# The first y tile of an interleave kernel: loaded by the store queue, issued ahead of the opening barrier

## Chip, cores, metric

The kernel runs on one core of one Trainium2 chip. The metric is the device time of one execution in microseconds (us), lower is better. All runs told of here were with a TensorE clock of 1.0 (TensorE does nothing in this kernel). Verdicts use a margin of 2%; several questions below are smaller than that, and for them the 95% interval of the ratio is given.

## The reference

```python
# x, y: float32 [32, 256, 1024]
result = np.zeros((32, 256, 2048), dtype=np.float32)
result[..., 0::2] = x
result[..., 1::2] = y
```

x and y are 33.55 MB each, the output 67.11 MB. There is no arithmetic: 134.2 MB are moved.

## The kernel before

The tensors are seen as flat. One tile is 128 partitions x 8192 floats (4.19 MB); there are eight of x and eight of y, in two buffers each. VectorE writes x into the even and y into the odd columns of an output tile, which is half as wide in inputs (4096 of each) and so is 4.19 MB too; there are sixteen, in two buffers. SP issues the loads, ACT the stores. The list of transfers that one issuing engine has handed over is called its queue or ring (q1 is SP's and q10 ACT's in the pages); both feed the same 16 DMA engines. A packet is what one DMA engine moves at a time, here a row of 32 KB. The opening barrier is the point where all engines wait for each other before the program's body.

```python
xpool = ctx.enter_context(tc.tile_pool(name="xp", bufs=2))
ypool = ctx.enter_context(tc.tile_pool(name="yp", bufs=2))
opool = ctx.enter_context(tc.tile_pool(name="op", bufs=2))
...
zero = wpool.tile([16, 128], fp32, name="zero")
nc.vector.memset(zero, 0.0)
first = dataclasses.replace(of, offset=0, ap=[[2 * WL, 16], [1, 128]])
nc.scalar.dma_start(out=first, in_=zero)          # the tiny write, 8 KB

for lw in lwidths:                                # 8 tiles
    ...
    nc.sync.dma_start(out=xtile, in_=xs)
    nc.sync.dma_start(out=ytile, in_=ys)
    soff = 0
    while soff < lw:                              # 2 output tiles
        ...
        nc.vector.tensor_copy(out=otile[:, 0::2], in_=xsub)
        nc.vector.tensor_copy(out=otile[:, 1::2], in_=ysub)
        nc.scalar.dma_start(out=os_, in_=otile)
        soff += width
```

After the program is built, the first x load is moved by hand into the program's opening block, ahead of SP's part of the opening barrier, so that it starts before the engines have met:

```python
at, moved = next((b, i) for b in blocks[1:] for i in b.instructions
                 if i.engine == mybir.EngineType.SP and i.opcode == "DMACopy")
assert not moved.sync_info.on_wait
... # take it out of its block
opening.insert(gate, moved)      # gate: SP's Drain in the opening block
```

The tiny write touches bytes that the first store overwrites; the first store waits for it.

## Time and profile before

| | before |
|---|---|
| time, median of 3 runs | 316.41 us (315.72 to 316.87) |
| span of the profiled run | 313.8 us |
| bytes moved, mean rate over the span | 134.23 MB, 428 GB/s |
| VectorE busy | 72.8 us, 23% |
| first store issued | 24.32 us after the span's start |

"Span" runs from the first to the last instruction on the device; it is about 1.8 us shorter than the time. A row of digits gives the busy tenths in 40 equal slices, 9 for 90% or more. In a timeline, "[11.25 <-DMA xtile<-in_x_dram]" says that the engine stood idle for 11.25 us and that the landing of this load ended it. A DMA's row stands at its issue, not where its data move. Most of the lines are in the prediction below; these two rows of the page give the copies, as busy us, mean ns | idle before:

```profile
L70 DVE COPY otile<-xtile 128x4096 f32<-128x4096 f32 x16 | 36.6, 2295 | 184.9 <-DMA out_dram<-otile 173.7
L71 DVE COPY otile<-ytile 128x4096 f32<-128x4096 f32 x16 | 36.6, 2292 | 39.8 <-DMA ytile<-in_y_dram 39.8
```

### The profile page before, as it was taken

The page shows a single profiled execution, that of the slowest core. Times are in us where ns is not written, and L with a number is a line of the kernel's source. Part 1 is how long each engine was busy: PE and PEld are TensorE (multiplying, and loading weights), DVE is VectorE, ACT ScalarE, POOL GpSimd, SP SyncE. Part 2 cuts the span into 40 slices and gives each one's busy share as a digit, 9 for nine tenths or more (in the row PEclk, how much of TensorE's full clock was granted, in tenths as well). Part 3 has the DMA queues.
Part 4 walks back from the last instruction along what each step waited for, and adds up shares of the span by engine and source line. Part 5 has one row for each costly group of instructions (what it writes and reads, how often), then busy time and mean ns, then how long its engine had stood idle before and what let it go on. Part 6 is the DMA issues. An engine that isn't in the chain of part 4 may idle for free.

```text
span 313.8 us, 152 instructions
## 1 busy us (share of the span) xinstructions
DVE 72.8 (23%) x33; POOL 0.2 (0%) x4
## 2 busy tenths in 40 slices
DVE  0433002231032410325003150130501305023500
POOL 0000000000000000000000000000000000000000
DMA  8999999999999999999999999999999999999997
GB/s 339 464 405 397 468 401 464 405 464 405 464 405 464 405 459 409 451 418 451 418 434 434 430 439 426 443 413 455 401 468 401 468 401 468 401 468 401 464 405 334
DMA packets 4640, 134.23 MB, mean 428 GB/s; under 512 B 528, under 2 KB 544, under 8 KB 544
## 3 DMA queue, kind: packets, MB, share of 16 engines
q1 hardware_dynamic: 2304, 67.11, 49.9%
q10 hardware_dynamic: 2336, 67.12, 49.5%
HBM read 67.11 MB, written 67.12 MB: 428 GB/s over the span
## 4 chain that ended last, share of the span: by engine, by line
DMA 83%; DVE 11%; DVEq 1%; issue 0%
DMA out_dram<-otile 76%; DMA ytile<-in_y_dram 7%; DVE otile L71 6%; DVE otile L70 5%; DVEq L83 1%; DVEq L70 0%
## 5 line engine op out<-in xcount | busy, mean ns | idle before, releaser
L70 DVE COPY otile<-xtile 128x4096 f32<-128x4096 f32 x16 | 36.6, 2295 | 184.9 <-DMA out_dram<-otile 173.7
L71 DVE COPY otile<-ytile 128x4096 f32<-128x4096 f32 x16 | 36.6, 2292 | 39.8 <-DMA ytile<-in_y_dram 39.8
L45 DVE MEMSET zero<- 16x128 f32 x1 | 0.2, 165 | 0.9 <-PEq L119 0.9
L119 POOL MEMSET const-bfloat16-1.0<- 128x1 bf16 x1 | 0.1, 102 | 0.0
L119 POOL MEMSET const-uint8-127<- 128x1 uint8 x1 | 0.1, 102 | 0.0
L119 POOL MEMSET const-float32-0.0<- 128x1 f32 x1 | 0.1, 99 | 0.2 <-issue 0.2
L119 POOL MEMSET const-float32-1.0<- 128x1 f32 x1 | 0.1, 99 | 0.0
## 6 DMA issues: line engine op xcount, KB each, us to landing
out_dram<-otile ACTq DMA_DIRECT2D x16, 4096.0 KB, 29.1
xtile<-in_x_dram SPq DMA_DIRECT2D x8, 4096.0 KB, 43.6
ytile<-in_y_dram SPq DMA_DIRECT2D x8, 4096.0 KB, 60.7
out_dram<-zero ACTq DMA_DIRECT2D x1, 8.0 KB, 6.3
```

The lines of the kernel that those rows point to most:

```text
L45: nc.vector.memset(zero, 0.0)
L70: nc.vector.tensor_copy(out=otile[:, 0::2], in_=xsub)
L71: nc.vector.tensor_copy(out=otile[:, 1::2], in_=ysub)
L83: tc.compile()
L119: nc = _bacc.Bacc("TRN2", target_bir_lowering=False, num_devices=1)
```

## The change

The intent: do for the first y load what was done for the first x load. It goes out on ACT's queue, which is empty at that time, ahead of ACT's part of the opening barrier; the tiny write comes after it on that queue.

```diff
-    nc.scalar.dma_start(out=first, in_=zero)
 ...
         nc.sync.dma_start(out=xtile, in_=xs)
-        nc.sync.dma_start(out=ytile, in_=ys)
+        yq = nc.scalar if start == 0 else nc.sync
+        yq.dma_start(out=ytile, in_=ys)
+        if start == 0:
+            nc.scalar.dma_start(out=first, in_=zero)
 ...
-    (the first DMACopy of SP is moved ahead of SP's Drain)
+    for engine in (mybir.EngineType.SP, mybir.EngineType.Activation):
+        (the first DMACopy of this engine is moved ahead of its Drain)
```

More of the change, by code (lines that the diff above doesn't have):

```diff
@@ L86 @@
     blocks = nc.main_func.blocks
-    opening = blocks[0].instructions
-    at, moved = next(
-        (b, i)
-        for b in blocks[1:]
-        for i in b.instructions
-        if i.engine == mybir.EngineType.SP and i.opcode == "DMACopy"
-    )
-    assert not moved.sync_info.on_wait
-    body = at.instructions
-    body.remove(moved)
-    gate = next(
-        n
-        for n, i in enumerate(opening)
-        if i.engine == mybir.EngineType.SP and i.opcode == "Drain"
-    )
-    opening.insert(gate, moved)
-    at.instructions = body
-    blocks[0].instructions = opening
+    for engine in (mybir.EngineType.SP, mybir.EngineType.Activation):
+        opening = blocks[0].instructions
+        at, moved = next(
+            (b, i)
+            for b in blocks[1:]
+            for i in b.instructions
+            if i.engine == engine and i.opcode == "DMACopy"
+        )
+        assert not moved.sync_info.on_wait
+        body = at.instructions
+        body.remove(moved)
+        gate = next(
+            n
+            for n, i in enumerate(opening)
+            if i.engine == engine and i.opcode == "Drain"
+        )
+        opening.insert(gate, moved)
+        at.instructions = body
+        blocks[0].instructions = opening
 _INS = ['x', 'y']
```

## The prediction

> **What bounds the kernel now.** I read the page first: rows of the 40 slices, then the queues, then the chain that ended last.
>
> ```profile
> span 313.8 us, 152 instructions
> DVE 72.8 (23%) x33; POOL 0.2 (0%) x4
> DMA  8999999999999999999999999999999999999997
> GB/s 339 464 405 397 468 401 464 405 464 405 464 405 464 405 459 409 451 418 451 418 434 434 430 439 426 443 413 455 401 468 401 468 401 468 401 468 401 464 405 334
> q1 hardware_dynamic: 2304, 67.11, 49.9%
> q10 hardware_dynamic: 2336, 67.12, 49.5%
> DMA 83%; DVE 11%; DVEq 1%; issue 0%
> ```
>
> VectorE, the only compute engine with work, is busy 23% of the span. The DMA row is 9 in 38 of 40 slices; only the first and the last are below. The two queues are the two issuing engines: q1 carries 67.11 MB, the bytes of x and y (the loads, issued by SP), q10 the output's 67.11 MB plus the tiny write (the stores, issued by ACT). Together they take 49.9 + 49.5 = 99.4% of the 16 engines' time. The chain says the same: 83% of it is DMA.
>
> Next I cut the span into stretches that end on events of the timeline, and asked for the DMA share and rate in each. Columns: start:end, length, VectorE busy (count), GpSimd busy (count), TensorE clock, DMA share, GB/s.
>
> ```profile
> 0.00:0.80 0.80, 0.00 (x0) 0.20 (x4) 1.00 0.00 0
> 0.80:12.28 11.48, 0.17 (x2) 0.00 (x0) 1.00 1.02 412
> 12.28:22.00 9.72, 4.50 (x3) 0.00 (x0) 1.00 1.00 432
> 22.00:48.11 26.11, 4.50 (x2) 0.00 (x0) 1.00 1.00 422
> 40.00:240.00 200.00, 45.44 (x20) 0.00 (x0) 1.00 1.01 435
> 287.67:311.80 24.13, 6.79 (x3) 0.00 (x0) 1.00 1.01 435
> 311.80:313.80 2.00, 0.00 (x0) 0.00 (x0) 1.00 0.00 0
> ```
>
> The reader is to see that the engines run at 435 GB/s in the middle, at 432 GB/s when one load ring alone is at work (12.28 to 22.00, the first y tile behind the first x tile), and at 435 GB/s when stores alone are (after the last load has landed at 287.67). So one ring is enough to fill the engines, and mixing directions neither helps nor hurts. 134.23 MB at 435 GB/s is 308.6 us; the span is 313.8, so 5.2 us are not carried at full rate. Of these 0.8 us pass before the first data packet, 2.0 us after the last one, 0.6 us are lost up to 12.28 (11.48 x (1 - 412/435)), 0.8 us in 22.00 to 48.11, where the first stores come in (26.11 x (1 - 422/435)), and about 1 us is spread.
>
> Last, the timeline of the opening, where the change lies (start, length, engine, line, operation, idle before it and who ended that).
>
> ```profile
> 0.00 0.37 SPq L56 DMA_DIRECT2D xtile<-in_x_dram  x1
> 0.78 0.33 SPq L57 DMA_DIRECT2D ytile<-in_y_dram  x1
> 1.06 0.42 ACTq L47 DMA_DIRECT2D out_dram<-zero  x1
> 1.16 0.42 SPq L56 DMA_DIRECT2D xtile<-in_x_dram  x1
> 1.63 0.51 SPq L57 DMA_DIRECT2D ytile<-in_y_dram  x1
> 12.28 4.50 DVE L70 COPY otile<-xtile 128x4096 f32<-128x4096 f32 x2 [11.25 <-DMA xtile<-in_x_dram]
> 16.80 0.33 SPq L56 DMA_DIRECT2D xtile<-in_x_dram  x1
> 22.00 4.50 DVE L71 COPY otile<-ytile 128x4096 f32<-128x4096 f32 x2 [5.22 <-DMA ytile<-in_y_dram]
> 24.32 2.56 ACTq L72 DMA_DIRECT2D out_dram<-otile  x2
> 26.52 0.33 SPq L57 DMA_DIRECT2D ytile<-in_y_dram  x1
> ```
>
> Four loads of 4.19 MB are in the SP ring by 2.1 us. At 432 GB/s each takes 9.7 us, so the ring holds work until about 41 us, and the third x load (16.80) and third y load (26.52) join long before that. The y load that the change brings forward is issued at 0.78, some 11.5 us before the x tile ahead of it has landed: its issue is not what it waits for.
>
> **What the Trainium skill says.** First, "DMA: Bandwidth & Descriptors", section "Issuing engines are not separate DMA queues": DMAs from scalar, sync or gpsimd all end on the same 16 engines and interleave, and issuing from several saves only the sequencer's issue time. The trace agrees as far as it can: issue takes 0.33 to 0.51 us against about 9.7 us of transfer. Second, same page, section "Queues, rings and completion order": each DMA engine takes turns between rings by packet, so two loads issued together on two rings should share each engine and finish together. The tiny write agrees that rings interleave: issued at 1.06 it landed 6.3 us after issue, inside the first x load, though that was far from done. Here 128 large packets of 32 KB make a tile, 8 for each engine. Third, same page, section "Where 436 GB/s comes from": a ceiling of 435.2 GB/s from 16 ports. The measured 435 GB/s sits on it, so I see no rate left to win in the middle of the span. Fourth, "HBM Reference", section "Specifications (TRN2)", gives about 358 GB/s for each core when its neighbour is busy too; the 428 GB/s mean over this span is above that, as the page says of a core streaming alone.
>
> **The change part by part.**
>
> 1. The first y load moves from third place (SP, 0.78) to the opening of ACT, about 0.0. Its issue comes 0.8 us earlier, but from 0.8 to 22.0 us the engines are filled by the x load alone already. Bytes moved earlier in total: none. What changes is who gets them. Until both are done they share, so both end near the time at which the second of them ends now: (0.8 us to the first packet) + 8.39 MB / 432 GB/s = 19.4 us, plus the 0.6 us of slow start and about 1.2 us from packet to semaphore (22.00 - 0.8 - 0.6 - 19.4), 22.0 us. I expect x to land at 21 to 22 us instead of 12.28, and y at 21.3 to 22.3.
>
> 2. The copies therefore begin at about 21.7 us instead of 12.28. The built program also orders them differently: before it is x, x, y, y for the two output tiles; after it is x, y, x, y. One copy is 2.25 us as they follow one another (4.50 for two). First output tile complete: 21.7 + 4.5 = 26.2 us against 24.3. Second: 30.7 us against 26.5. The first store is thus about 2 us later, the second about 4. This costs nothing by itself: the SP ring has two loads queued until 41 us if alone, and the engines do loads where they would have done stores.
>
> 3. Buffers come free later. The third x load waits for both copies of the first x tile: 21.7 + 3 x 2.25 = 28.5 us instead of 16.80; the third y load 30.7 instead of 26.52. Both are ahead of 41 us, and from 26 us stores halve the load rate, which postpones the moment further. The SP ring does not run dry.
>
> 4. The tiny write now stands behind y's packets in the ACT ring: landing near 22 us, some 21 us after its issue instead of 6.3. The first store waits for it (they write the same bytes), but that store is not ready before 26 us. Slack about 4 us. Cost: none.
>
> 5. ACT meets the opening barrier after its own issue, about 0.4 us; SP does the same already, beside it. If the barrier opened 0.4 us later, only the second x load and the memset would be later. Neither sets anything before 20 us.
>
> 6. The end: loads keep a lead of about 2 us x half the rate, 0.4 MB, over stores compared with now. They finish 1 to 3 us earlier and stores run alone so much longer, at the same 435 GB/s. The last wait for an output buffer costs a pair of copies, 4.5 us, while the other 4.19 MB store runs for 9.6 us: still covered.
>
> Sum: 0 in the middle, 0 at the end, between -0.7 and 0 at the start. The gain possible there is the 0.6 us of slow start: after the first round of 16 packets near 1.0 us the next round starts near 2.9 us, later rounds follow each 1.2 us. A second ring could put packets into that first gap. I take about a quarter of it, -0.2 us: 316.4 - 0.2 = 316.2 us.
>
> **The rivals.**
>
> Rival 1, a real gain: the x and y loads together end earlier, because a single ring leaves the engines underfilled. For it: the first slice has 339 GB/s, and the first x tile takes 12.28 us against 9.72 for the y tile after it. Against it: of these 2.6 us most is fixed time to first packet and to the semaphore, and the same single ring does 432 GB/s right after. Its most is the 1.4 us up to full rate, most of it latency: time 315.0 to 315.8 us.
>
> Rival 2, a loss through the later start: x arrives 9 us later, VectorE sits idle until 21.7 instead of 12.28, stores start 2 to 4 us later. If stores were the bound, this would be the full shift: 318 to 320 us. Against it: the chain's first store and everything after it moves at the pace of shared engines, which have other work during the delay; full store rate after the last load makes up for it.
>
> Rival 3, a loss of rate: reading x and y in lockstep from two distant regions could disturb memory, and the first stores' entry costs 0.8 us now. If the first 21 us ran 5% slower, it would be +1.0 us, 317.4. Against it: loads and stores run side by side from two regions for 200 us at 435 GB/s.
>
> **Range and chances.** Three runs of before spread over 315.72 to 316.87, 1.15 us. Around 316.2 I allow -1.0 for noise with rival 1 and +1.1 for noise with rival 3: 315.2 to 317.3. To be 2% faster the kernel would have to end below 310.1, which is within 2 us of carrying all bytes at 435 GB/s with no start and no end; 1% for that. To be 2% slower takes 6.3 us of idle engines, more than the whole shift in the stores; 1%. The rest, 98%, is within 2%.
>
> **What would show it right or wrong.** Right: the first x copy starts at 21 to 22.5 us with an idle time of 20 to 21 us before it; the first y copy no longer waits 5.2 us but under 0.7; q1 falls to 62.92 MB and q10 rises to 71.31 MB (4.19 MB change sides); the tiny write lands about 21 us after issue; the third x load is issued near 28.5; the DMA row keeps its 9s and the rate up to 22 us stays at 390 to 415 GB/s; steady copies follow in pairs with a period of 38.7 us; the last load lands 1 to 3 us earlier. Wrong: x landing near 12 us (rings that do not share evenly), a slice below 9 between 20 and 50 us (a ring that ran dry), a rate below 425 GB/s in 40 to 240, or a last store that ends after a gap.

## The result, and the profile after

| | before | after |
|---|---|---|
| time, median of 6 runs each | 316.15 us (315.67 to 316.87) | 316.04 us (315.79 to 316.44) |
| ratio after / before | | 0.9996, interval 0.998 to 1.0012 |
| the changed kernel once more, later, beside 11 runs of before | 315.83 us | 316.05 us, ratio 1.0002, interval 0.999 to 1.0014 |

A ratio is the mean time of one kernel's fast runs over the mean of the other's fast runs of the same rounds, so it is not quite the ratio of the medians quoted. The change moves the time by less than 0.2% either way.

The page of the changed kernel: span, DMA row, the queues (packets, MB, share of the 16 engines), the chain by engine, and the rows of the x and y copies.

```profile
span 314.3 us, 151 instructions
DMA  9999999999999999999999999999999999999997
q10 hardware_dynamic: 2480, 71.31, 52.6%
q1 hardware_dynamic: 2160, 62.92, 46.9%
DMA 82%; DVE 12%; DVEq 1%; issue 0%
L72 DVE COPY otile<-xtile 128x4096 f32<-128x4096 f32 x16 | 36.7, 2294 | 224.5 <-DMA out_dram<-otile 203.9
L73 DVE COPY otile<-ytile 128x4096 f32<-128x4096 f32 x16 | 36.7, 2291 | 0.6
```

4.19 MB have gone over from the load queue to the store queue, and nothing else: the engines are as full as before. The y copies wait 0.6 us in total, where before they waited 39.8. A wait of 39 us has vanished and the time has not moved. It came back elsewhere: the x copies now wait 203.9 us for stores to free output buffers, against 173.7, and the first of them waits 9.3 us longer for its load (20.6 against 11.3).

The same stretches as in the prediction, in the changed kernel (start:end, length, VectorE, GpSimd, clock, DMA share, GB/s):

```profile
0.80:12.28 11.48, 0.17 (x1) 0.00 (x0) 1.00 1.00 411
12.28:22.00 9.72, 0.23 (x1) 0.00 (x0) 1.00 1.00 432
22.00:48.11 26.11, 8.67 (x4) 0.00 (x0) 1.00 1.02 421
40.00:240.00 200.00, 45.44 (x20) 0.00 (x0) 1.00 1.00 433
287.67:311.80 24.13, 4.83 (x3) 0.00 (x0) 1.00 1.01 435
```

Before, these read 412, 432, 422, 435 and 435. (The 433 against 435 is no more than one packet for each of the 16 engines, 0.5 MB, at the edge of a window of 200 us.) The two loads, side by side on two rings, moved no more in the first 12 us than one load on one ring had.

The opening of the changed kernel in its timeline (the first row merges the first and the second x load, at 0.00 and about 0.9):

```profile
0.00 1.25 SPq L55 DMA_DIRECT2D xtile<-in_x_dram  x2
0.12 0.38 ACTq L57 DMA_DIRECT2D ytile<-in_y_dram  x1
1.20 0.39 ACTq L59 DMA_DIRECT2D out_dram<-zero  x1
21.77 2.30 DVE L72 COPY otile<-xtile 128x4096 f32<-128x4096 f32 x1 [20.60 <-DMA xtile<-in_x_dram]
23.98 2.29 DVE L73 COPY otile<-ytile 128x4096 f32<-128x4096 f32 x1
26.18 2.28 DVE L72 COPY otile<-xtile 128x4096 f32<-128x4096 f32 x1
26.30 29.73 ACTq L74 DMA_DIRECT2D out_dram<-otile  x3
28.49 0.33 SPq L55 DMA_DIRECT2D xtile<-in_x_dram  x1
30.69 0.33 SPq L57 DMA_DIRECT2D ytile<-in_y_dram  x1
```

y is issued 0.66 us earlier than before (0.12 against 0.78) and lands at the same time (issued at 0.12 and landing 21.8 us later, so at 21.9, against 22.00). x, which had landed at 12.28 us, lands at 21.74 now: it has given half of the engines to y. The first store goes out 2 us later (26.30 against 24.32), the third x load 11.7 us later (28.49 against 16.80). None of it costs time, because the loads already issued last until about 40 us (39.8 us in the run with six copies of delay below).

### The profile page after: what moved, and what is told of

It is laid out like the page before. It is cut to its first block, busy times and chain, and to the rows that moved or that the text cites. A ratio compares the mean times of both kernels' runs of the same rounds, so it can differ in the third digit from the quotient of the medians.

```text
span 314.3 us, 151 instructions
## 1 busy us (share of the span) xinstructions
DVE 72.7 (23%) x33; POOL 0.2 (0%) x4
## 4 chain that ended last, share of the span: by engine, by line
DMA 82%; DVE 12%; DVEq 1%; issue 0%
DMA out_dram<-otile 75%; DMA xtile<-in_x_dram 7%; DVE otile L72 7%; DVE otile L73 6%; DVEq L85 1%; DVEq L72 0%
## 5 line engine op out<-in xcount | busy, mean ns | idle before, releaser
L72 DVE COPY otile<-xtile 128x4096 f32<-128x4096 f32 x16 | 36.7, 2294 | 224.5 <-DMA out_dram<-otile 203.9
## 6 DMA issues: line engine op xcount, KB each, us to landing
ytile<-in_y_dram ACTq DMA_DIRECT2D x1, 4096.0 KB, 21.8
```

## The experiments

Theory A: the end is set by the time of the first packet plus all bytes at 435 GB/s. Which ring carries a load, and when a store gets ready, does not matter as long as the engines have something to move. Its rivals: the early issue is worth its own time; a second ring fills the engines better at the start; and a late first store delays the end. Edits are against the changed kernel unless said otherwise.

### What the opening is worth: nothing early

```diff
-        yq = nc.scalar if start == 0 else nc.sync
+        yq = nc.sync
-    for engine in (mybir.EngineType.SP, mybir.EngineType.Activation):
+    for engine in ():
```

> Both first loads on the SP ring, both behind the opening barrier (the first x load's head start is undone too). Theory A (the end is set by the first packet's time plus all bytes at 435 GB/s): the first packet comes about 0.8 us later, since SP's first load behind the barrier was issued at 0.78 us in the kernel before, so about +0.8 us, 316.9 us, ratio to before 1.0025. Theory B (the opening does not matter at all at this size): 316.1 us, ratio 1.000.

Measured: 316.83 us against 315.81, ratio 1.0031 (1.0019 to 1.0043). Its timeline:

```profile
0.73 0.36 SPq L55 DMA_DIRECT2D xtile<-in_x_dram  x1
13.27 4.50 DVE L72 COPY otile<-xtile 128x4096 f32<-128x4096 f32 x2 [12.29 <-DMA xtile<-in_x_dram]
```

The first load is issued at 0.73 us, its first packet starts at 1.72 us instead of 0.99 (read from the kept packet lists), and its copies start at 13.27 instead of 12.28. The time grows by 1.0 us (interval 0.6 to 1.4), where 0.8 was expected. So a later first packet, 0.73 us, is paid in full; the other 0.3 us are within the noise. The trick played on the first x load in the kernel before is worth 0.3%. There is only one first packet: the second load cannot earn it again.

### The early issue alone: y on SP's ring, ahead of the barrier

```diff
-        yq = nc.scalar if start == 0 else nc.sync
+        yq = nc.sync
-    for engine in (mybir.EngineType.SP, mybir.EngineType.Activation):
+    for engine in (mybir.EngineType.SP, mybir.EngineType.SP):
```

> The early issue alone: the first y load is issued ahead of the opening barrier, but on the SP ring behind the x load. Theory A: nothing, 316.1 us, ratio 0.999 to 1.001; the x tile lands at about 12.3 us and the y tile at 22.0, as in the kernel before, so the late landing of x in the changed kernel belongs to the second ring. Theory B (early issue is worth its 0.8 us): 315.4 us, ratio 0.9975.

Measured: 316.06 us, ratio 1.0003 (0.9991 to 1.0015). y is issued at 0.42 us, x's copies start at 12.42 and y's at 22.15, as in the kernel before. Theory B's 0.9975 is outside the interval. The late landing of x in the changed kernel is therefore the work of the second ring, not of the early issue.

### The second ring alone: y on ACT's ring, behind the barrier

```diff
-    for engine in (mybir.EngineType.SP, mybir.EngineType.Activation):
+    for engine in (mybir.EngineType.SP,):
```

> The second ring alone: the first y load on the ACT ring, but behind the barrier, ahead of the tiny write. Theory A: nothing, 316.1 us, ratio 0.999 to 1.001; x lands at 20.5 to 22 us although y is issued about 1 us after it. Theory B (a second ring fills the gap of the first packets): the mean rate from 0.8 to 12.28 us rises above 425 GB/s and the time falls by 0.5 us.

Measured: 316.68 us, ratio 1.0038 (1.0015 to 1.0061), with one run of six at 318.86. Theory B falls: 411 GB/s from 0.8 to 12.28 us, as in the changed kernel (before: 412), and no gain in time. Theory A's "nothing" is missed as well. The opening, in the timeline:

```profile
19.48 2.29 DVE L72 COPY otile<-xtile 128x4096 f32<-128x4096 f32 x1 [18.45 <-DMA xtile<-in_x_dram]
24.34 2.29 DVE L73 COPY otile<-ytile 128x4096 f32<-128x4096 f32 x1 [2.57 <-DMA ytile<-in_y_dram]
```

y, issued at 0.77, comes in 2.4 us later than in the changed kernel, x 2.3 us earlier. I ran the same kernel again, with the changed kernel beside it:

> The second ring without the early issue, once more, because its first reading was 0.4% slower than before, with one of six runs at 318.86 us, where theory A said nothing. Theory A (the slow reading was chance): ratio to before 0.999 to 1.001, and within 0.2% of the changed kernel run beside it here. Theory C (a y load that starts about a packet later than x on the other ring is a real loss): ratio 1.002 to 1.004 again, and slower than the changed kernel beside it.

> The changed kernel itself, unchanged, as the measure of what repeats: ratio to before 0.998 to 1.002.

Measured: 316.86 us for this kernel, ratio 1.0043 (1.0008 to 1.0079), again with one slow run of six, 320.62; 316.05 us for the changed kernel, ratio 1.0002 (0.999 to 1.0014). Without the one far run in each, the means are still 0.7 us above before. So a loss of 0.7 to 0.8 us repeats, and in each set one run lost several us more. The slow run happened to be the profiled one.

The four kernels make a two-by-two of ring and issue. On SP's ring the early issue is worth nothing (316.06 us against 315.81), but on ACT's ring it is worth about 0.8 us (316.05 against 316.86). So the change is neutral as a whole, while the second ring without the early issue loses.

Theory A has no term for this loss, so I looked at the sixteen parts of each transfer. The Trainium skill, "DMA: Bandwidth & Descriptors", section "Why a DMA increments its semaphore by 16 and not by 1", says that each of the engines taking part adds one when its own share has landed. The trace agrees: it holds 528 such increments for 33 transfers, 16 each (512 for 32 without the tiny write). The time from the first to the last of the 16 says how far apart the engines end; I call it the spread. For the last store of each profiled run (worked out from the recorded increments):

```
kernel                              span    spread   span - spread
before                              313.8   0.45     313.4
after                               314.3   0.52     313.8
after, again                        314.3   0.69     313.6
after without the tiny write        314.1   0.48     313.6
after, two copies of delay          314.0   0.45     313.6
y early on SP's ring                314.3   0.83     313.5
y late on ACT's ring, first         314.4   0.78     313.6
y late on ACT's ring, slow run      318.8   3.56     315.2
before without the tiny write       314.6   1.11     313.5
every y on ACT's ring               315.2   1.86     313.3
nothing early                       315.3   0.81     314.5 (first packet 0.7 later)
```

Ten of the eleven rows give 313.3 to 313.8 in the last column once the later first packet is taken off. What differs among kernels that move the same bytes is how far the slowest engine ends behind the first. In the slow run the spread of the tiny write and the stores grew in steps until about 173 us, stayed there until 289 us, and part of it closed at the end: 0.53 us at the tiny write, 3.23 at the transfer landing near 53 us, 5.04 near 75, 6.72 near 173, 3.56 for the last store. That names where most of the slow run's 4.4 us went (2.8 of them are spread; 1.6 are not). A spread in mid run is no measure of a loss: the changed kernel run again shows 1.92 us from 35 to 287 us, ends with 0.69, and lost nothing (316.12 us).

The kept traces say a little more. In the slow run fourteen of the sixteen parts of the last store landed within 0.18 us, the other two 2.05 and 3.56 us after the first. A packet takes 1.21 us as a rule (the median of all), but 19 packets of stores that started between 46 and 70 us took 1.34 to 1.68 us. That fits one or two engines held up by slow packets. What slows these packets, and why this kernel is more prone to it, stays open; so does the cause of the 0.8 us in its ordinary runs, of which only one has a trace, with a spread of 0.78.

### The tiny write

```diff
-        if start == 0:
-            nc.scalar.dma_start(out=first, in_=zero)
```

In the kernel before, the same one line is taken out.

> The changed kernel without the tiny write. Theory A: no change, 316.0 us: the y load now opens the ACT ring, the tiny write's 8 KB are 0.02 us at 435 GB/s, and its landing at 24.2 us was before the first store at 26.3. Theory B (a small transfer among large packets disturbs the engines, or the first store waits for it): 0.3 to 1 us faster, ratio 0.997 to 0.999.

> The kernel before without the tiny write. If the tiny write pays for opening the ACT ring ahead of the first store, the first store lands later and the time rises, ratio 1.001 to 1.003. Theory A (the SP ring has loads until 41 us, so a slow opening of the ACT ring is hidden): ratio 0.999 to 1.001.

Measured: in the changed kernel 316.0 us without it, ratio to before 1.0006 (0.9994 to 1.0018): no effect. In the kernel before 316.36 us without it, ratio 1.0014 (1.0002 to 1.0026). That is a loss of 0.5 us, just clear of noise. It came as the first half of the expectation had it, against theory A: the first store is issued at 24.21 us without it and 24.32 with it, yet its buffer is free at 50.00 instead of 48.11. But the later landing alone does not explain the loss, since the next experiment shows that a store 8.9 us later costs nothing. In the end the spread is 1.11 us instead of 0.45, which is more than the loss. How the missing tiny write leads to that spread is not shown.

### A late first store: two copies of delay, and six

```diff
+        if start == 0:
+            for _ in range(2):          # or 6
+                nc.vector.tensor_copy(out=xtile, in_=xtile)
```

> The changed kernel with two copies of the first x tile onto itself ahead of the interleaving (right result). Such a copy is put at about 4.4 us (twice the 2.25 us of a half tile), so the first store comes at about 35 us instead of 26.3, while the SP ring still has loads until about 40 us. Theory A (late stores are free while the engines have loads): 316 us, ratio 0.998 to 1.003. Rival 2 of the prediction (a late first store delays the end by as much): about 325 us, ratio 1.028.

> The same with six such copies: the first store comes at about 53 us, but the two loads in the SP ring are done at about 40 us and the third x load waits for the copies too. Theory A: the engines sit idle from about 40 to 53.5 us, and just that is added: 316 + 13 = 329 us, ratio 1.036 to 1.046, with slices of the DMA row below 9 there. Rival 2: the full delay of 26.4 us, about 342 us, ratio 1.083.

Two copies: 316.17 us, ratio 1.0007 (0.9993 to 1.0022). The first store went out 8.9 us later than in the changed kernel, and it cost nothing:

```profile
35.15 4.77 ACTq L77 DMA_DIRECT2D out_dram<-otile  x2
```

Six copies: 331.65 us, ratio 1.0495 (1.0481 to 1.0509). The first store was issued at 53.08 us. The DMA row, and the stretch without a packet:

```profile
DMA  9999805999999999999999999999999999999996
39.80:53.60 13.80, 13.70 (x5) 0.00 (x0) 1.00 0.00 0
```

The added time is 15.8 us (over the 315.83 of before), not the 26.8 us by which the first store was late. 13.8 us of it are the hole in which no packet starts; the last store's spread was 1.94 us against 0.52 to 0.69, which is about 1.3 more; some 0.7 us are left, about what the slow start cost at the beginning (0.6 us), though that it is the same thing is only argued. The expectation of 13 us had the hole nearly right and missed the rest. So rival 2 of the prediction falls in both runs, and the edge is where theory A has it: lateness is free until the load ring is empty, at about 40 us, and then it costs what the engines stand idle.

### The bytes themselves: a load left out at the start, or at the end

```diff
+        ytile = xtile if start == 0 else ypool.tile(...)    # or: start == total - P * lw
+        if start != 0:                                      # the same condition
             yq.dma_start(out=ytile, in_=ys)
```

In the first of the two the second early issue goes as well, since there is no y load to move. The results are wrong: one tile interleaves x with x.

> The disputed transfer taken away altogether (a wrong result on purpose: the first tile interleaves x with itself). First stores start near 17 us. Theory A: 4.19 MB less at 435 GB/s is -9.6 us: 306.5 us, ratio 0.9695. If instead the wait of the first copies on that load were what counts: first store 9.3 us earlier than in the changed kernel with the bytes gone besides, more than 9.6 us, down to 300 us. If hidden: 316 us.

> The changed kernel with the last y load taken away instead of the first (a wrong result on purpose). Theory A: the same -9.6 us, 306.5 us, within 0.7 us of the run without the first y load: a load's price is its bytes, wherever it stands. If waits at the opening counted, the two would differ by several us. It could fall short if stores alone at the end cannot keep the engines full (a wait of 4.5 us for each pair of copies); then 307 to 311 us.

Measured: 306.33 us without the first y load, ratio 0.97 (0.9687 to 0.9712); 306.48 us without the last, ratio 0.9702 (0.9688 to 0.9716). That is 9.50 and 9.35 us less than the 315.83 of before, where 4.19 MB at 435 GB/s are 9.6 us. Without the first y load the first store went out at 16.75 us, 9.6 us before that of the changed kernel, and this earned nothing on top. A load's price is its bytes, at the start and at the end alike.

### The change taken further: every y load on ACT's queue

```diff
-        yq = nc.scalar if start == 0 else nc.sync
+        yq = nc.scalar
```

> The change taken further: every y load on the store queue. Theory A with both rings always holding work: the bytes are the same, ratio 0.998 to 1.003. But the ACT ring is in order, so the first store stands behind the second y load and the third y load is issued after the fourth store: if that leaves the engines without work, or VectorE without a free buffer while both rings run dry, some us more, up to 325 us, with slices of the DMA row below 9.

Measured: 317.72 us (316.61 to 319.88), ratio 1.0068 (1.004 to 1.0095): above theory A's 1.003, far below 325. Two lines of its timeline:

```profile
61.38 2.29 DVE L72 COPY otile<-xtile 128x4096 f32<-128x4096 f32 x1 [30.68 <-DMA out_dram<-otile]
75.95 1.06 ACTq L57 DMA_DIRECT2D ytile<-in_y_dram  x2
```

As feared, the third y load is only issued at 75.95 us (30.69 in the changed kernel), behind the fourth store, and VectorE waits 30.68 us for the first store, which stands in the ring behind a y load. But the DMA row of this run (316.99 us) has no slice below 9 before the last: the rings never ran dry. It ends with a spread of 1.86 us, 1.4 more than before, and 1.4 us is also its difference from before in the span. Fifteen of the sixteen parts landed within 0.50 us, and one at 1.86; three packets of this run, at 232.5, 234.4 and 273.3 us, took 1.71, 1.40 and 2.05 us instead of 1.21, together 1.5 us more. So the loss of the profiled run fits a few slow packets on one engine, and not the order of the loads. The spreads of the slower runs of this kernel are not known.

## Why the prediction was right

The predicted 316.2 us against a measured 316.04, inside the range of 315.2 to 317.3. The mechanism was right: no bytes earlier, waits that only change places. That the number is as close as 0.16 us is luck: it started from 316.41, the median of three runs of before, where six give 316.15, and took off a gain of 0.2 us that does not show. Point by point:

1. "Bytes moved earlier in total: none." Right. x landed at 21.74 us (21 to 22 predicted) and y at 21.9 (21.3 to 22.3). The two rings share the engines evenly, as the prediction drew from the Trainium skill ("DMA: Bandwidth & Descriptors", section "Queues, rings and completion order"): in the packet list, 16 packets of x start from 1.01 us, 16 of y from 2.77, 16 of x from 3.98, and so on. The runs with y early on SP's ring and late on ACT's ring show that the sharing comes from the ring alone.
2. The copies and first stores: 26.30 us for the first (26.2 predicted), about 30.7 for the second. "This costs nothing by itself" is shown by the run with two copies of delay, where a store 8.9 us later still cost nothing.
3. The third x load at 28.49 (28.5), the third y load at 30.69 (30.7); the SP ring does not run dry. Right: no slice is below 9 before the last. The run with six copies shows what it would have cost otherwise.
4. The tiny write landed 23.0 us after issue (some 21 predicted), at 24.2, ahead of the first store at 26.30. Right, with 2 us of slack rather than 4; taking it out changed nothing.
5. ACT's barrier: VectorE's memset began at 1.00 us against 0.86, and nothing came of it.
6. The last load landed at 285.7 us (issued at 229.71, landing 56.0 us later) against 287.67, 2.0 us earlier where 1 to 3 was predicted, and the stores alone kept 435 GB/s.

One term of the sum rested on a wrong reading: the -0.2 us for a second ring that fills the gap between the first round of packets near 1.0 us and the next near 2.9. There is no gap. Packets, MB and share of the 16 engines, from 0 to 2 us and from 2 to 3.7 us, before:

```profile
q1 hardware_dynamic: 16, 0.52, 95.8%
q1 hardware_dynamic: 16, 0.52, 71.5%
```

and after:

```profile
q1 hardware_dynamic: 16, 0.52, 87.1%
q10 hardware_dynamic: 16, 0.52, 71.6%
```

A round is 16 packets for 16 engines, so the share times the window is the time of one packet: 1.92 us in the first round before and 1.74 after, 1.22 us in the second. The engines are busy with the long first packet all that time. y, issued at 0.12 us, gets its first packet at 2.77 us, just where x's second round had stood (2.86). Both loads are in at 21.92 us instead of 21.97. So 0.05 us is what the trace shows of the term; a gain of 0.2 us in the time could not be told from noise. (The first packet starts at 0.99 us, not at the 0.8 of the prediction; its sum to 22.0 us is not affected, since its last part was taken from the 22.00 itself.) Rival 1, 0.6 us or more, thus falls, rival 2 falls by the delay runs, and rival 3 (a loss of rate by two regions read at once) does not show: 411 and 412 GB/s up to 12.28 us, and 432 from there to 22 us in both kernels.

The prediction had no term for the engines ending apart. It did not matter for this change (0.45 us before, 0.52 and 0.69 after), but it is larger than the term that I argued about.

## What to carry to other kernels

When the DMA engines are full from the first packet to the last, as here, the time is set by the bytes (9.4 to 9.5 us for 4.19 MB) and by the first packet (1.0 us when it came 0.73 us later); fewer bytes or an earlier first packet are what is left to try. Moving one load to another queue ahead of the barrier only changed who waits (ratio 0.9996); doing it behind the barrier, or with every y load, lost 0.4 to 0.7%, for a reason that is open. A wait that vanishes from VectorE (39 us here) is no gain if the engines were busy during it; ask instead when the rings would run dry. Among variants that differ by less than a per cent, look at how far apart the sixteen parts of the last transfer land, and at packets that took longer than the rest, before explaining the difference by the schedule.

## What the Trainium skill lacked or had wrong

- "DMA: Bandwidth & Descriptors", section "Queues, rings and completion order": no figure is given for how far the engines of one core end apart in a long run, or how that differs from run to run. The runs that move all bytes show 0.45 to 3.56 us between the first and the last part of the last store, and up to 6.74 us in the middle of the slow run.
- The same page gives no figure for the longer first packets of a run: 1.92 us (1.74 in the changed kernel) where the packets of the next round took 1.22.
- The same page, section "Issuing engines are not separate DMA queues": right that the issuing engine gives no bandwidth (ratio 0.9996, and 411 against 412 GB/s). That section does not say (though the one on queues and rings lets one work it out) that splitting two loads over two queues makes the first of them land later (21.74 us instead of 12.28), nor does the page say that it can cost a little: 0.4% with y late on ACT's ring, 0.7% with every y load there.
- I found no page that gives the worth of an early first DMA for a kernel of this kind. The runs show 1.0 us of 316 for issuing the first load ahead of the opening barrier, and nothing for the second on the same queue.
